# A decoder layer on eight cores: stages around the norms in two column parts, with bf16 weight copies, spread norm steps and independent stores

## The chip, the cores and the metric

The kernel runs one program on all 8 cores of one Trainium2 chip (two dies, cores 0 to 3 and 4 to 7). Each core has 1024 of the 8192 tokens and the whole set of weights. The metric is device time in microseconds (us) of the slowest core, from its first to its last instruction.

The program has a fast and a slow state. In a slow run the cores of one die, sometimes of both, show a lower granted TensorE clock than the others, and the run is up to 20 % longer. A run is called slow when one die is over 1 % longer than the other at a lower clock, or when it is over 1.5 % above the fastest run of the same kernel. Fast runs are compared with fast runs. Where a profile was taken in a slow run, only cores of the die that kept its clock are read, and the text says so.

The engines are TensorE (PE in the profile; PEld is its weight load), VectorE (DVE), ScalarE (ACT), GpSimd (POOL) and SyncE (SP). On the pages a DMA transfer is issued from the queue of an engine, in the kernel before the 688 loads of up weights from GpSimd's (POOLq) and the 32 output stores from SyncE's (SPq).

## The reference, cut to what matters

```python
D_MODEL, SEQ, D_FF, PLE_DIM = 4096, 8192, 11008, 256      # 32 q heads, 4 kv heads of 64, window 128

h = rms_norm(x, norm_mix_pre)
z = h @ w_in                                   # q | k | v | u | g_attn | g_pool
y_attn = sliding_window_attention(q, k, v, sinks) @ w_branch_attn
y_pool = multiscale_pool(u, w_pool, pool_scale) @ w_branch_pool
merged = sigmoid(g_attn) * y_attn + sigmoid(g_pool) * y_pool
x = x + rms_norm(merged @ w_out, norm_mix_post)             # norm after "out"

h = rms_norm(x, norm_ffn_pre)                               # norm before "up"
up = causal_depthwise_conv(h @ w_up, conv_w, conv_b)        # width 3
gate, val = split(up, 2)
x = x + rms_norm((gelu(gate) * val) @ w_down, norm_ffn_post)     # norm after "down"

g = sigmoid(rms_norm(x, norm_ple_gate) @ w_ple_gate)        # norm before "pg"
x = x + rms_norm(g * (p @ w_ple), norm_ple_post)            # last norm: the tail
```

An RMS norm needs the sum of squares over all 4096 channels of a token before any channel can be scaled. On this kernel channels are chunks (32 of 128) and tokens are columns. So between two matmul stages with a norm between them, the last chunk of the first stage has to be done before the first matmul of the second can start, for the same columns.

I use short names for the stages, in order: kv, q (with the attention under it), u (with the pooling), gate (with both branch projections), out, up1, down1, up2, down2, up3, down3 (the MLP in three slices of its 86 chunks), pg (ple gate), tail.

## The kernel before

A small scheduler records every operation with the buffers it reads and writes and turns them into semaphore waits. Each operation waits for the last writer of what it reads, and for the last writer and all readers of what it writes.

```python
def op(self, eng, meth, kw, reads=(), writes=(), dma=None, partial=False):
    deps = {}
    for b in reads:
        ...  # deps of b.w
    for b in writes:
        for d in (b.w, b.r):
            for k, v in d.items():
                if deps.get(k, 0) < v:
                    deps[k] = v          # also where partial=True
    ...
    for b in writes:
        if partial:
            b.w[key] = tid
        else:
            b.w = {key: tid}
            b.r = {}
```

Weights lie in HBM as f32. They are loaded in slabs of 8 x 128 x 128 through a ring of 12 buffers by a DMA from GpSimd's queue that casts to bf16. A job walks over its slabs; for each of the K steps it issues one matmul per column block, here three of 342 columns (1026 in all), with one weight load each.

```python
for kk in range(nk):
    k = k0 + kk
    if job["kpre"] and ci == 0:
        job["kpre"](k)                       # work that has to precede this k step
    ...
    for h, bk in enumerate(ch["banks"]):
        self.O("pe", "matmul", [self.wringB[i]] + rb, [self.psB[bk]], partial=not first,
               out=self.ps[:, bk, 0:ch["n"]], lhsT=self.wring[i][:, kk * 128:(kk + 1) * 128],
               rhs=ch["rhs"](k, h), start=first, stop=last)
    ...
    if job["side"] and cnt // job["side"] > (cnt - 1) // job["side"] and self.side:
        self.side.popleft()()                # side work, here the attention
```

The start, for each of four slabs of 296 columns: all 8 statistics steps (square on ACT, sum by matmul, scaling on DVE), then the K/V matmuls of that slab.

The attention of a chunk of two heads is queued as side work when its q chunk is evicted. Letters are score steps (A, B, one for each head) and value steps (P, Q for this chunk, p, q for the chunk before):

```python
def evac_q(f=f, banks=banks):
    tri_mul(G["q"][f % 3], ...)              # DVE: q rows, 1026 columns
    for c in "A0 p1 B0 A1 q1 B1 A2 p2 B2 q2 A3 B3 P0 A4 B4 Q0".split():
        ...                                  # append the step to B.side
```

The norm between out and up (the one between down and pg is built the same way) is the `kpre` of the first up chunk, over all 1026 columns:

```python
def bar1_k(k):
    ...
    bar1_load()                              # residual rows, 3 buffers in turn
    O("dve", "tensor_tensor", ...)           # m *= rstd
    O("dve", "scalar_tensor_tensor", ...)    # m = m * gain + residual
    O("act", "activation", ..., func=AF.Copy, scale=gains[:, 2, k:k + 1])   # h1[k], bf16
    O("act", "activation", ..., func=AF.Square)
    O("sp", "dma_start", [mB], [x1B[k]], ...)            # store x1
    if n < RESID0:
        O("sp", "dma_start", [msB[n]], [mB], ...)        # fetch a spilled chunk
    tok_ss(...)                              # 9 one-column matmuls: sums of squares per token
```

The tail, after the last matmul, over all 1024 columns and 32 chunks:

```python
outB = Buf("out")
...
for n, f in enumerate(order):
    xload(n + 3)                             # residual x2, 512 KB
    if f < nsp:
        O("sp", "dma_start", [r3B[f]], [rB_], ...)       # spilled result back, 512 KB
    ...
    O("dve", "tensor_tensor", ...)           # r *= rstd
    O("dve", "scalar_tensor_tensor", ...)    # r = r * gain + x2
    O("sp", "dma_start", [rB_], [outB], partial=True, dma="out", out=out_d[f], in_=r)
```

The softmax here doesn't subtract the row's maximum and nothing guards it: scores larger than these inputs give would overflow.

Of the kernel before, what the change touches and what calls it, by code (L numbers as in the profile page):

```python
# [18 lines left out]
H3 = 342  # L19
NK = 1184  # L20
OFF_E = 158
OFF_U = 143
NU = 1041
U3 = 347
NSL = 4
SL = 296
SPLITS = (34, 34, 18)
# [3 lines left out]
RESID0 = 8  # L31
NXS = 3
SCRATCH = 4096

# [119 lines left out]

class Builder:
    def __init__(self):
        nc = self.nc = bass.Bass("TRN2", target_bir_lowering=False, dynamic_dma_scratch_size=SCRATCH)
        self.S = Sched(nc)
        self.live = []
        self.jobs = []  # L160
        self.side = deque()

# [4 lines left out]
    def tile(self, name, off, shape, dt):  # L167
        n = 1
        for s in shape:
            n *= s  # L170
        nb = n * (4 if dt == F32 else 2)
        assert off % 4 == 0 and nb % 4 == 0 and off + nb <= self.arena_bytes, (name, off, nb, self.arena_bytes)
        b = Buf(name)
        b.lo, b.hi = off, off + nb
        keep = []
        for o in self.live:
            if o.lo < b.hi and b.lo < o.hi:
                o.dead = True
                for d in (o.w, o.r):
                    for k, v in d.items():  # L180
                        if b.r.get(k, 0) < v:
                            b.r[k] = v
                if not (b.lo <= o.lo and o.hi <= b.hi):
                    keep.append(o)
            else:
                keep.append(o)
        keep.append(b)
        self.live = keep
        return self.view(off, shape, dt), b


    def tiles(self, name, off, n, shape, dt):
        e = 1
        for s in shape:
            e *= s
        nb = e * (4 if dt == F32 else 2)
        bs = [self.tile(f"{name}_{i}", off + i * nb, shape, dt)[1] for i in range(n)]
        return self.view(off, [n] + list(shape), dt), bs

    def view(self, off, shape, dt):  # L200
        nb = 4 if dt == F32 else 2
        for s in shape:
            nb *= s
        v = self.arena[:, off // 2:(off + nb) // 2]
# [4 lines left out]
        elif len(shape) == 3:  # L209
            v = v.rearrange("p (a b c) -> p a b c", a=shape[0], b=shape[1])  # L210
        return v


    def slabs(self, wname, chunk, sizes, K, base=0):
# [3 lines left out]
        for n in sizes:  # L218
            out.append((wname, off, n, k0))
# [4 lines left out]
    def mm(self, chunks, slabs, side=0, kpre=None, pre=None):  # L224
        self.jobs.append(dict(chunks=chunks, slabs=slabs, side=side, kpre=kpre, pre=pre))
# [4 lines left out]
    def chunk(self, banks, n, K, rhs, rb, evac):  # L230
        return dict(banks=banks, n=n, K=K, rhs=rhs, rb=rb, evac=evac, done=0)

    def load_next(self):
        if self.nload >= len(self.allslabs):
            return
        wname, off, nk, k0 = self.allslabs[self.nload]
        i = self.nload % NS
        self.nload += 1
        src = self.dram[wname][off:off + nk * 16384].rearrange("(p m) -> p m", p=128)
        self.O("pool", "dma_start", [], [self.wringB[i]], dma=f"wr{i}", out=self.wring[i][:, 0:nk * 128], in_=src)  # L240

    def run_jobs(self):
        self.allslabs = [s for j in self.jobs if "slabs" in j for (ci, s) in j["slabs"]]
        self.nload = 0
        self.ncons = 0
        for job in self.jobs:
            if "fn" in job:
# [4 lines left out]
            cnt = 0  # L252
            for ci, (wname, off, nk, k0) in job["slabs"]:
# [5 lines left out]
                for kk in range(nk):  # L259
                    k = k0 + kk  # L260
                    if job["kpre"] and ci == 0:
                        job["kpre"](k)
                    first, last = ch["done"] == 0, ch["done"] == ch["K"] - 1
                    rb = ch["rb"](k)
                    for h, bk in enumerate(ch["banks"]):
                        self.O("pe", "matmul", [self.wringB[i]] + rb, [self.psB[bk]], partial=not first,
                               out=self.ps[:, bk, 0:ch["n"]], lhsT=self.wring[i][:, kk * 128:(kk + 1) * 128],
                               rhs=ch["rhs"](k, h), start=first, stop=last)
                    ch["done"] += 1
                    cnt += 1  # L270
                    if job["side"] and cnt // job["side"] > (cnt - 1) // job["side"] and self.side:
                        self.side.popleft()()
# [9 lines left out]
def build_nc():  # L282
    B = Builder()
    nc, O = B.nc, B.O

# [3 lines left out]
    def dscr(name, shape, dt=F32):  # L289
# [4 lines left out]
    pT_d = din("pT", [128, 2 * T])  # L294
    B.dram = dict(
        w_in=din("w_in", [D * 12800]), w_pool=din("w_pool", [4 * 512 * 512]), w_ba=din("w_ba", [2048 * D]),
        w_bp=din("w_bp", [2048 * D]), w_out=din("w_out", [D * D]), w_up=din("w_up", [D * 2 * DFF]),
        w_down=din("w_down", [DFF * D]), w_pg=din("w_pg", [D * D]), w_ple=din("w_ple", [256 * D]))
    gains_d = din("gains", [128, 6 * NCH])
    conv_d = din("convp", [128, 172 * 4])  # L300
    pscale_d = din("pscale", [128, 16])
    sinks_d = din("sinks", [128, 16])
    corr_d = din("corr", [128, 4 * 18])
    mask_d = din("mask", [128, 512], BF16)
    mask0_d = din("mask0", [128, 132], BF16)
    identb_d = din("identb", [128, 128], BF16)
    out_d = nc.dram_tensor("out", [NCH, 128, T], F32, kind="ExternalOutput").ap()
    mg_d = dscr("mg_s", [30, 128, NE], BF16)
    ms_d = dscr("mix_s", [RESID0, 128, NE])
    x1_d = dscr("x1_s", [NCH, 128, T])  # L310
    yp_d = [dscr(f"yp{i}_s", [NCH, 128, T]) for i in range(2)]
    x2_d = dscr("x2_s", [NCH, 128, T])
    r3_d = dscr("r3_s", [16, 128, T])

    st = ExitStack()
    with st:
        def sb(name, shape, dt):
# [4 lines left out]
        gains = sb("gains", [128, 6, NCH], F32)  # L322
        convp = sb("convp", [128, 172, 4], F32)
        pscale = sb("pscale", [128, 16], F32)
        esink = sb("esink", [128, 16], F32)
        corr = sb("corr", [128, 4, 18], F32)
        maskn = sb("maskn", [128, 512], BF16)
        mask0 = sb("mask0", [128, 132], BF16)
        identb = sb("identb", [128, 128], BF16)
# [3 lines left out]
        sst = sb("sst", [128, 9], F32)  # L333
        rA = sb("rA", [128, NK], F32)
        diag = [sb("diag0", [128, 128], F32)[:], rA[:, 1028:1156]]
        rB = sb("rB", [128, NE], F32)
        constB, sstB, rAB, rBB = Buf("const"), Buf("sst"), Buf("rA"), Buf("rB")
        diagB = [Buf("diag0"), Buf("diag1")]
        B.arena_bytes = ((nc.sbuf_bytes_remaining if not callable(nc.sbuf_bytes_remaining)
                          else nc.sbuf_bytes_remaining()) - 64) // 64 * 64  # L340
        B.arena = sb("arena", [128, B.arena_bytes // 2], BF16)
        ps = B.ps = st.enter_context(nc.psum_tensor("ps", [128, 8, 512], F32))
        psB = B.psB = [Buf(f"ps{i}") for i in range(8)]
        tile = B.tile


        def ld(dst, src):
            O("sp", "dma_start", [], [constB], partial=True, dma="cst", out=dst, in_=src)

        ld(gains[:].rearrange("p a b -> p (a b)"), gains_d)  # L350
        for dst, src in ((pscale[:], pscale_d), (esink[:], sinks_d), (corr[:].rearrange("p a b -> p (a b)"), corr_d),
                         (maskn[:], mask_d), (mask0[:], mask0_d), (identb[:], identb_d),
                         (convp[:].rearrange("p a b -> p (a b)"), conv_d)):
            ld(dst, src)
# [3 lines left out]
        O("dve", "memset", [], [sstB], ap=sst[:], constant=1.0)  # L358

        def tri(b0, n=H3):  # L360
            return ps[:, b0:b0 + 3, 0:n]
# [7 lines left out]
        TRI = ((0, 1, 2), (3, 4, 5))  # L369
        trc = [0]  # L370

        def next_tri():
            trc[0] ^= 1
            return TRI[trc[0]]

        PAIRS = ((0, 1), (2, 3), (4, 5), (6, 7))
        prc = [0]

        def next_pair():
            prc[0] = (prc[0] + 1) % 4  # L380
            return PAIRS[prc[0]]

        def bufs(banks):
            return [psB[b] for b in banks]
# [935 lines left out]
```

## Time and profile before

| | |
|---|---|
| runs of the listing | 7780.94, 8340.58 and 7171.13 us; median 7780.94 |
| profiled run (fast), core by core | 7145 to 7193 us |
| TensorE busy on the slowest core | 6692 of 7193 us |

Two of the three listed runs are slow. The fast time is 7171.

The page of the slowest core (core 1) starts with the busy time of each engine and the span in 40 equal slices. A digit is the busy share of a slice in tenths, PEclk is the granted TensorE clock in tenths.

```profile
...
PE 6692.4 (93%) x41700; PEld 4047.1 (56%) x41700; DVE 1885.3 (26%) x1931; ACT 757.9 (11%) x937; POOL 1035.7 (14%) x1943
...
PE   6889999999999968999999999999999999977980
...
PEclk9999999999999987999999999999999999988995
DMA  6334555555569555444446654444577644677546
...
```

TensorE is above 90 % in most slices. The dents are at the start, at slices 15 and 16, at slice 36, and in the last two. The chain of work that ended last, from the same page, agrees:

```profile
...
PE 91%; DMA 6%; DVE 2%; ACT 1%; issue 1%; SPq 0%; POOL 0%; DVEq 0%; ACTq 0%; POOLq 0%
...
```

For the sizes I cut the span of core 3, which ran undisturbed, at the borders of the stages. The borders come from counting matmuls in program order in the trace. The rows of this table of windows are: start, q, u, gate, out, the 174 us after out, the middle, the 175 us after down3, the rest of pg, tail. Columns: the window, its length, then busy time (and instructions) of PE, PEld, DVE, ACT, POOL, then the clock, the DMA share and GB/s.

```profile
...
0.00:168.30 168.30, 100.23 (x660) 66.23 (x661) 56.14 (x173) 42.77 (x45) 28.02 (x34) 0.93 0.66 164
168.30:526.60 358.30, 318.94 (x2186) 202.52 (x2184) 122.55 (x282) 169.37 (x350) 33.28 (x63) 0.95 0.30 47
526.60:796.60 270.00, 260.62 (x1740) 170.15 (x1739) 95.14 (x105) 30.10 (x46) 40.11 (x76) 0.99 0.44 67
796.60:2157.50 1360.90, 1359.51 (x9266) 901.72 (x9264) 201.46 (x165) 73.27 (x69) 204.81 (x388) 1.00 0.55 86
2157.50:2625.60 468.10, 455.28 (x3090) 301.26 (x3087) 45.61 (x38) 72.32 (x70) 68.09 (x129) 0.99 0.56 90
2625.60:2800.00 174.40, 87.26 (x632) 50.14 (x632) 89.90 (x82) 70.66 (x71) 6.85 (x13) 0.62 0.73 225
2800.00:6384.70 3584.70, 3567.71 (x21697) 2115.62 (x21696) 1004.25 (x860) 160.88 (x153) 573.29 (x1086) 1.00 0.54 94
6384.70:6560.00 175.30, 119.77 (x645) 50.12 (x646) 92.18 (x83) 78.14 (x77) 17.44 (x33) 0.72 0.84 240
6560.00:6957.20 397.20, 391.42 (x1801) 176.71 (x1798) 99.22 (x81) 57.07 (x54) 63.90 (x121) 0.99 0.49 83
6957.20:7154.00 196.80, 0.00 (x0) 0.00 (x0) 78.62 (x64) 3.46 (x3) 0.00 (x0) 0.50 0.59 192
...
```

Length minus PE busy is TensorE's idle time: 68 us in the start, 39 in q, 9 in u, 87 after out, 56 after down3, 197 in the tail, 37 in the rest. Together 493 us of 7154. Where TensorE comes and goes, the mean clock of the window falls too (0.62 and 0.72 in the two norm windows). Part of that fall is the idle time itself, which is recorded at 0.50 (the last row, where TensorE is busy for 0.00 us), so how much the lower clock adds to the cost of the norms was not worked out.

On core 1, the slowest one, 162 us right after the first norm (from 2784.7 us on) ran at a clock of 0.81; core 3 has no such stretch. This makes part of the dent at slice 16 of the page above and of the 39 us by which core 1 is longer.

What a norm waits for is told by the chain of waits of core 1, in order of time (start, duration, what):

```profile
...
2701.76 6.88 DMA sb_arena<-xr
...
2708.73 1.30 DVE sb_arena L138
...
2710.50 7.20 DMA sb_arena<-xr
```

A residual load of 7 us lands, one VectorE operation follows, then the next load is issued and takes 7 us. The loads and the arithmetic take turns. The norm after down3 has the same pattern with loads of 4 to 6 us.

In the attention the hole stands at each q eviction. The timeline of core 1 (start, duration, engine, operation; in brackets the idle time before it and who ended it):

```profile
...
367.33 0.56 DVE L138 TENSOR_TENSOR sb_arena<-ps,sb_arena 64x386 bf16<-64x386 f32 x1 [1.89 <-ACT sb_arena L138]
367.92 1.23 DVE L138 TENSOR_TENSOR sb_arena<-ps,sb_rA 128x1026 bf16<-128x1026 f32 x1
...
369.40 0.32 PE L138 MATMUL ps<-sb_arena 128*128 128x130 bf16 x2 [2.71 <-DVE sb_arena L138]
...
371.42 1.92 PE L138 MATMUL ps<-sb_arena,sb_wr 128*128 128x342 bf16 x6
...
```

The q eviction (1.23 us) waits in VectorE's queue behind a multiply of the step before it, and the first score matmuls wait for it, 2.71 us. Six 342-column matmuls then take 1.92 us, where six such took 1.04 us a little earlier in the same trace. The granted clock is 0.50 for 3.4 us from 370.3 us on, and 1.00 before and after. The array had been idle for 2.71 us before the score matmuls. What sets the moment of the fall is not shown.

In the tail about two thirds of the chain is DMA; VectorE has 18 % of it:

```profile
...
7007.14 3.68 DMA out<-sb_arena
...
7010.89 4.28 DMA out<-sb_arena
...
7095.55 5.38 DMA sb_arena<-r_s
...
```

### The profile page before, as it was taken

Reading aid. Unit: us, or ns where it says so; the run is one execution under the profiler, and the core shown is the slowest. Engines: PE = TensorE matmul, PEld = TensorE weight load, DVE = VectorE, ACT = ScalarE, POOL = GpSimd, SP = SyncE. Lnnn points to the kernel's source line nnn. Section 1 sums busy time; section 2 is a strip of 40 time slices with the busy share of each in tenths; the row PEclk is TensorE's granted clock in tenths of the full one; section 3 lists DMA queues with packets and bytes.
Section 4 is the critical chain, followed back from the end, with each engine's and each line's share of the span. In section 5 each row is a group of like instructions: output and inputs, shape, how many; then the busy total and the mean of one; then the engine's idle time right before and its main releaser. Section 6 shows DMA issues by size and latency. Waiting matters only on the chain.

```text
span 7193.1 us, 100231 instructions; the slowest of 8 cores (7145.0 to 7193.1 us)
## 1 busy us (share of the span) xinstructions
PE 6692.4 (93%) x41700; PEld 4047.1 (56%) x41700; DVE 1885.3 (26%) x1931; ACT 757.9 (11%) x937; POOL 1035.7 (14%) x1943
## 2 busy tenths in 40 slices
PE   6889999999999968999999999999999999977980
PEld 4556666666666644666664456666644566433440
DVE  3333211111110024333330013333300233343223
ACT  2441000000001122000000000000000000122110
POOL 1001111111111100111111111111111111111110
PEclk9999999999999987999999999999999999988995
DMA  6334555555569555444446654444577644677546
GB/s 155 48 45 67 77 81 82 82 82 81 81 113 120 75 127 160 70 75 75 75 78 113 111 96 76 75 75 75 89 148 151 109 75 75 122 183 169 95 68 202
DMA packets 343309, 711.99 MB, mean 99 GB/s; under 512 B 38736, under 2 KB 57424, under 8 KB 340816
## 3 DMA queue, kind: packets, MB, share of 16 engines
q0 software_dynamic: 278928, 480.90, 45.7%
q1 hardware_dynamic: 63936, 224.68, 9.4%
q8 instruction: 338, 5.54, 0.3%
q14 instruction: 107, 0.88, 0.0%
HBM read 1083.94 MB, written 102.26 MB: 165 GB/s over the span
## 4 chain that ended last, share of the span: by engine, by line
PE 91%; DMA 6%; DVE 2%; ACT 1%; issue 1%; SPq 0%; POOL 0%; DVEq 0%; ACTq 0%; POOLq 0%
PE ps L138 91%; DVE sb_arena L138 2%; DMA sb_arena<-x_s 1%; DMA out<-sb_arena 1%; DMA sb_arena<-r_s 1%; DMA sb_arena<-xr 1%; DMA x_s<-sb_arena 1%; DMA sb_arena<-w_in 1%; ACT sb_arena L138 1%; DMA sb_arena<-xs 0%; POOL sb_arena L138 0%; SPq L138 0%; DMA sb_wr<-w_pg 0%; ACT sb_rA L138 0%; ACT L138 0%
## 5 line engine op out<-in xcount | busy, mean ns | idle before, releaser
L138 PE MATMUL ps<-sb_arena,sb_wr 128*128 128x342 bf16 (+2 forms) x39744 | 6504.5, 325 | 28.4 <-ACT sb_arena L138 20.7
L138 PEld LDWEIGHTS ps<-sb_arena,sb_wr 128*128 128x128 bf16 x39744 | 3887.3, 98 | 2533.3 <-issue 44.7
L138 ACT ACTIVATE sb_arena<-sb_arena 128x1024 bf16<-128x1024 f32 (+7 forms) x470 | 443.9, 948 | 4795.6 <-DVE sb_arena L138 4689.9
L138 DVE TENSOR_TENSOR sb_arena<-ps,sb_rB 128x1026 f32<-128x1026 f32 (+1 forms) x204 | 250.2, 1226 | 2201.0 <-PE ps L138 2201.0
L138 POOL DMA_DIRECT2D sb_wr<-w_up x688 | 363.2, 528 | 2213.0 <-PE ps L138 2042.9
L138 DVE TENSOR_TENSOR sb_arena<-ps,sb_arena 128x1024 f32<-128x1024 f32 (+4 forms) x256 | 245.1, 958 | 1121.0 <-PE ps L138 951.5
L138 DVE SCALAR_TENSOR_TENSOR sb_arena<-sb_arena,sb_convp 128x1024 f32<-128x1024 f32 x344 | 442.0, 1285 | 37.7 <-DVE sb_arena L138 2.3
L138 DVE TENSOR_TENSOR sb_arena<-sb_arena 128x1024 bf16<-128x1024 f32 (+6 forms) x251 | 308.4, 1229 | 525.7 <-ACT sb_arena L138 499.9
L138 POOL DMA_DIRECT2D sb_wr<-w_in x384 | 203.0, 535 | 1384.7 <-PE ps L138 1316.7
L138 DVE TENSOR_TENSOR sb_arena<-ps,sb_rA 128x1026 f32<-128x1026 f32 (+4 forms) x136 | 136.6, 1004 | 1008.8 <-PE ps L138 1008.0
L138 POOL DMA_DIRECT2D sb_wr<-w_down x416 | 219.6, 528 | 1001.8 <-PE ps L138 921.7
L138 ACT ACTIVATE sb_arena<-ps 128x512 bf16<-128x512 f32 (+6 forms) x259 | 154.4, 596 | 987.3 <-PE ps L138 980.8
L138 PE MATMUL ps<-sb_arena 128*128 128x296 bf16 (+3 forms) x1216 | 185.9, 275 | 55.3 <-DVE sb_arena L138 45.3
L138 PEld LDWEIGHTS ps<-sb_arena 128*128 128x128 bf16 x1216 | 113.2, 102 | 133.7 <-issue 95.8
L138 DVE SCALAR_TENSOR_TENSOR sb_arena<-sb_arena,sb_gains 128x1024 f32<-128x1024 f32 (+1 forms) x96 | 123.4, 1285 | 132.9 <-DMA sb_arena<-x_s 63.7
L138 PE MATMUL ps<-sb_ones_b,sb_arena 128*128 128x1 bf16 x544 | 25.4, 165 | 142.7 <-ACT sb_arena L138 142.7
L138 DVE TENSOR_SCALAR sb_arena<-sb_arena,sb_convp 128x1024 f32<-128x1024 f32 x172 | 139.9, 814 | 19.6 <-DVE sb_arena L138 1.5
L138 DVE TENSOR_TENSOR sb_arena<-sb_arena,sb_rA 128x1024 f32<-128x1024 f32 (+1 forms) x96 | 117.2, 1220 | 103.9 <-DMA sb_arena<-r_s 81.1
L138 PEld LDWEIGHTS ps<-sb_ones_b,sb_arena 128*128 128x128 bf16 x544 | 21.6, 101 | 183.3 <-issue 181.9
L138 POOL DMA_DIRECT2D sb_wr<-w_out x128 | 67.6, 528 | 383.6 <-PE ps L138 362.6
L138 POOL DMA_DIRECT2D sb_wr<-w_pg x128 | 67.6, 528 | 267.9 <-PE ps L138 245.9
L138 PE MATMUL ps<-sb_arena,sb_ones_b 128*128 128x296 bf16 x128 | 27.0, 355 | 61.5 <-ACT sb_arena L138 33.7
(42 smaller groups left out, 462.9 us busy)
## 6 DMA issues: line engine op xcount, KB each, us to landing
sb_wr<-w_up POOLq DMA_DIRECT2D x688, 256.0 KB, 3.6
sb_wr<-w_in POOLq DMA_DIRECT2D x384, 256.0 KB, 4.3
sb_wr<-w_down POOLq DMA_DIRECT2D x320, 256.0 KB, 4.6
sb_wr<-w_out POOLq DMA_DIRECT2D x128, 256.0 KB, 4.1
x_s<-sb_arena SPq DMA_DIRECT2D x64, 512.0 KB, 5.0
yp_s<-sb_arena SPq DMA_DIRECT2D x64, 512.0 KB, 6.7
sb_arena<-yp_s SPq DMA_DIRECT2D x64, 512.0 KB, 5.5
sb_wr<-w_pg POOLq DMA_DIRECT2D x128, 256.0 KB, 4.4
```

Of the source, the lines that this page charges most:

```text
L138: inst = getattr(engine, fn[0])(**fn[1])
```

## The change

The intent:

1. **Two column parts around a norm.** out, the first 20 up chunks, down3 and pg run once over columns 0 to 511 and then over the rest, so that one part's norm can run under the other part's matmuls. The weights of these stages are therefore read twice.
2. **bf16 copies of those weights.** 116 casting DMAs, spread under the earlier stages, write them to HBM, and the part stages read the copies: half the bytes.
3. **Norm steps spread and pipelined.** A norm is a list of up to 37 small steps, popped one every 14 to 24 k steps. Within a step the multiply, the add, the store and the sum of squares belong to different chunks, and six residual buffers are loaded ahead. Sums of squares become 512-column matmuls.
4. **Statistics of the next K/V slab under the matmuls of the present one**, constants in two loads on another queue.
5. **The attention order**: the first thing after a q eviction is a value step of the chunk before.
6. **Aligned column blocks**: 344, 344, 338 (u: 352, 352, 338; full up: 512, 264, 250) in buffers padded so that every moving operand starts at a multiple of 16 bytes.
7. **The tail** has only the second column part; each output store has an entry of its own, 22 residual chunks are loaded early, nothing is spilled. The MLP is split 29, 29, 28 instead of 34, 34, 18.

```diff
-H3 = 342
+NP = 1032
+H3 = 344
+W3 = (H3, H3, NE - 2 * H3)
-SPLITS = (34, 34, 18)
+SPLITS = (29, 29, 28)
+PARTS = ((0, ((0, 512),)), (504, ((0, 264), (264, 258))))
+RU = 20
...
+    def cast_next(self):
+        dst, do, src, so, n, b = self.casts.popleft()
+        self.O("pool", "dma_start", [], [b], dma=f"cw{self.ncast % 8}", out=self.dram[dst][do:do + n]..., in_=...)
...
+                    if side:
+                        self.due += 1 / side
+                        if self.due >= 1:
+                            self.due -= 1
+                            if self.side:
+                                self.side.popleft()()
...
+        h0 = [alloc(f"h0_{c}", [NK], BF16, shift=4) for c in range(NCH)]
...
+                    if k % 15 == 14 and B.side:              # next slab's statistics
+                        B.side.popleft()()
...
-                for c in "A0 p1 B0 A1 q1 B1 A2 p2 B2 q2 A3 B3 P0 A4 B4 Q0".split():
+                for c in "p1 A0 q1 B0 A1 p2 B1 A2 q2 B2 A3 P0 B3 A4 Q0 B4".split():
...
+        def norm_steps(n, blocks, src, rstd, gp, res, put, gn, hout, rn, xs=None, later=0):
+            ...
+            def step(i):
+                def run():
+                    for lag, fn in ((0, scaled), (1, added), (2, done), (4, ss)):
+                        if 0 <= i - lag < NCH and (hout is not None or fn is not ss):
+                            fn(i - lag)
+                    ...
+            return [start] + [step(i) for i in range(NCH + (4 if hout is not None else 2))]
...
+                    B.side.extend(bar1(hf, G["acc"]))        # after the part's last out chunk
...
-                O("sp", "dma_start", [rB_], [outB], partial=True, dma="out", out=out_d[f], in_=r)
+                b = Buf(f"out{hf}_{k}")
+                outB.append(b)
+                O("sp", "dma_start", [m.b], [b], dma=f"out{k % 8}", out=out_d[k][:, t0:t0 + 512], in_=m.v)
```

(The arena allocator and the renaming of buffers, the larger part of the lines, are cut.)

## The prediction

> All times are for fast runs (before: 7171 us, profiled core 7193); slow runs are not what I predict.
>
> **What bounds it now.** TensorE. The page's busy line gives PE 6692 of 7193 us, the chain of waits is 91% PE. In the table of windows the middle (900 to 2520, 3060 to 6120 us) is dense at clock 1.00. Two things can be won: idle stretches, and ns per matmul.
>
> Idle, from the chain and timeline (core 1):
> - start: the last K/V matmul ends at 166 us for about 80 us of PE work; each 296-column slab's statistics run before its matmuls, not under them.
> - attention under the q projection (186 to 561): 23.5 us per chunk against 17.4 us of PE work. Each chunk has a 5 us hole (363 to 369 us): the q eviction (1.23 us) queues behind the last softmax multiplies, then matmuls run at half clock for about 3 us.
> - out to up norm (2616 to 2775) loses about 145 us; down to gate norm (6402 to 6542) about 115. Each chunk waits for a load, two DVE operations and an ACT square.
> - tail: last matmul 7000, end 7193; 6 us for each of 32 chunks.
>
> Rate: 342-column matmuls start 144 or 148 ns apart in a fixed pattern, 512-column ones 215.8.[...] 347 columns cost about 150.
>
> **What the change does.**
> - Aligns reads: 344+344+338[...] (estimate 144.5 each); u 352+352+338; up 512+264+250 (estimate 436.5 for three, now 440.6). Over 512 q, 512 u, 2048 gate, 1024 branch and 4864 full up k-steps: -48 us, all on the path.
> - Norms in two column parts, steps spread under the other part's matmuls: takes back nearly all of 145+115 us. Adds 28 us of 512-column sums of squares.
> - Part stages need a weight slab every 1.7 us: 152 GB/s, against 75 now. bf16 copies halve the reads; 116 casting copies (2 MB read, 1 MB written each) hide under earlier stages, DMA share there rising from 0.5 to 0.7-0.8.
> - Start: pipelined statistics; DMA (about 34 MB) then binds; q starts near 145, not 170.
> - Attention order: hole per chunk 1-2 us, about -65 us.
> - Tail: half the columns, 22 of 32 residual chunks loaded early: 32 x 1.27 us DVE + 8 us, about 50, not 193: -143 us.
>
> Sum: PE work after, estimate 6490 us at full clock. Plus start idle 65, attention 30, stage boundaries 10, tail 50, part-stage DMA stalls 20, slowest core 15.
>
> **Predicted: 6680 us, range 6600 to 6860. Faster by over 2%: 0.95; within 2%: 0.035; slower: 0.015.**
>
> **Right if** PE is busy about 97%, clock near 1.00 in all slices but the first three; no slice below 9 at the old norm places; last matmul to end about 50 us; 344-column matmuls about 144.5 ns apart.
>
> **Wrong if** part stages are DMA-bound (weights 152 GB/s plus norm loads and stores up to 150 GB/s come near saturation; PE would wait on the weight ring), or casting copies delay weight loads by more than the ring's 12 slabs, or the denser kernel draws a lower clock even in its fast state.

Sum: 6490 + 65 + 30 + 10 + 50 + 20 + 15 = 6680 us. The -48 us of aligned reads, which are within the 6490, rest on my estimates of 144.5 and 436.5 ns alone. The spacings of 144 or 148 and 440.6 ns are measured; that aligned reads would take about the shorter one was not shown at that time. The 17.4 us of TensorE work per chunk are an estimate too; the spacings in the trace of the kernel before (core 3) give about 17.6 (96 x 146.7 + 24 x 109 + 16 x 55 ns). For "near saturation", that trace has 306 GB/s at a DMA share of 0.93 (core 3, 2700 to 2750 us).

## The result, and the profile after

In one session on one chip the changed kernel ran 6697.12, 6669.98, 6669.40 (fast) and 7984.99 us (slow), median 6683.55. The kernel before ran 7171.13 and 7171.16 (fast), 7780.94 and 8340.58 (slow), median 7476.05. Ratios in this document are the mean time of one kernel's fast runs over that of the other's of the same rounds, so not quite the ratio of the medians that are quoted. Here it is 0.931, with a 95 % interval of 0.926 to 0.937: 6.9 % less.

A second series on another occasion gave 6670.78 to 6672.59 us in its four fast runs and a ratio of 0.9295 [0.9275, 0.9314]. Its profile is used for the sizes, since no core was disturbed.

The page of the slowest core of the first series (core 4, 6695.6 us), the same lines as before:

```profile
...
PE 6561.1 (98%) x41283; PEld 4030.5 (60%) x41283; DVE 1975.1 (29%) x2585; ACT 828.2 (12%) x1248; POOL 1352.8 (20%) x2531
...
PE   6999999999999999999999999999999999999996
...
PEclk9998999999999999999999999999999999999998
DMA  7557988899887587688899988556875555589885
...
```

```profile
...
PE 95%; DMA 1%; DVE 1%; ACT 1%; issue 1%; POOL 0%; DVEq 0%; ACTq 0%; SPq 0%; POOLq 0%
...
```

All the dents but the first and the last are gone, and the DMA digits are higher nearly everywhere. The table of windows of the second series, core 7, with these rows: start, q, u, gate, out, all of the MLP, pg, tail.

```profile
...
0.00:145.50 145.50, 95.03 (x655) 65.27 (x656) 57.98 (x181) 43.33 (x45) 29.18 (x42) 0.91 0.82 197
145.50:458.50 313.00, 300.37 (x2188) 195.34 (x2186) 122.87 (x281) 169.04 (x350) 37.45 (x71) 1.00 0.52 81
458.50:722.30 263.80, 256.89 (x1743) 169.29 (x1741) 95.84 (x106) 30.20 (x47) 44.83 (x85) 0.99 0.70 103
722.30:2067.00 1344.70, 1343.25 (x9265) 906.25 (x9263) 202.41 (x165) 73.60 (x69) 230.02 (x436) 1.00 0.77 121
2067.00:2526.00 459.00, 457.31 (x3110) 304.10 (x3109) 85.66 (x128) 122.44 (x197) 137.89 (x257) 1.00 0.66 184
2526.00:6132.00 3606.00, 3600.67 (x22117) 2164.19 (x22116) 1157.28 (x1341) 256.54 (x334) 705.85 (x1331) 1.00 0.70 132
6132.00:6620.70 488.70, 480.59 (x2218) 217.06 (x2215) 212.93 (x319) 132.19 (x206) 166.19 (x310) 1.00 0.77 226
6620.70:6667.20 46.50, 0.09 (x1) 0.00 (x0) 40.56 (x64) 1.32 (x2) 0.00 (x0) 0.51 0.47 181
...
```

TensorE's idle time is now 50 us in the start, 13 in q, 7 in u, 1 in gate, 2 in out, 5 in the MLP, 8 in pg and 46 in the tail: 133 us of 6667, where it was 493 of 7154. Stage by stage, counted from the matmuls in the trace, in us (start and u of the changed kernel are from core 7 of the first series, which ran undisturbed there too; in the second series they are 145.8 and 263.5):

| stage | before, core 3 | after, core 7 | difference |
|---|---|---|---|
| first instruction to first q matmul | 168.3 | 145.5 | -22.8 |
| q with attention | 358.3 | 313.0 | -45.3 |
| u with pooling | 270.0 | 263.7 | -6.3 |
| gate and branches | 1360.9 | 1344.9 | -16.0 |
| out | 468.1 | 458.6 | -9.5 |
| up, three slices | 2555.5 | 2408.9 | -146.6 |
| down, three slices | 1203.5 | 1197.6 | -5.9 |
| pg | 572.5 | 488.5 | -84.0 |
| tail | 196.9 | 46.4 | -150.5 |
| span | 7154.1 | 6667.2 | -486.9 |

In the timeline (core 4 of the first series) the q eviction still takes 1.23 us, but it now lies under other work. Six matmuls of q run while it runs, and the next score matmuls wait 0.39 us:

```profile
...
342.38 1.23 DVE L144 TENSOR_TENSOR sb_arena<-ps,sb_arena 128x1032 bf16<-128x1032 f32 x1
...
342.44 1.03 PE L144 MATMUL ps<-sb_arena,sb_wr 128*128 128x344 bf16 x6
...
343.87 0.32 PE L144 MATMUL ps<-sb_arena 128*128 128x130 bf16 x2 [0.39 <-DVE sb_arena L144]
...
```

And the tail's chain (same core) is VectorE with two operations per chunk, one chunk every 1.26 us:

```profile
...
6650.76 0.75 DVE sb_arena L144 x2
6652.63 0.74 DVE sb_arena L144 x2
...
```

### The profile page after: what moved, and what is told of

Its sections match the earlier page's. It is cut to its first block, busy times and chain, and to the rows that moved or that the text cites. A ratio compares the mean times of both kernels' runs of the same rounds, so it can differ in the third digit from the quotient of the medians.

```text
span 6695.6 us, 104771 instructions; the slowest of 8 cores (6662.8 to 6695.6 us)
## 1 busy us (share of the span) xinstructions
PE 6561.1 (98%) x41283; PEld 4030.5 (60%) x41283; DVE 1975.1 (29%) x2585; ACT 828.2 (12%) x1248; POOL 1352.8 (20%) x2531
## 4 chain that ended last, share of the span: by engine, by line
PE 95%; DMA 1%; DVE 1%; ACT 1%; issue 1%; POOL 0%; DVEq 0%; ACTq 0%; SPq 0%; POOLq 0%
PE ps L144 95%; DVE sb_arena L144 1%; ACT sb_arena L144 1%; DMA sb_arena<-w_in 1%; DMA sb_arena<-xs 1%; POOL sb_arena L144 0%; DVEq L143 0%; ACTq L143 0%; ACT L144 0%; DVEq L132 0%; ACT sb_warm L144 0%; SPq L143 0%; POOLq L169 0%
## 5 line engine op out<-in xcount | busy, mean ns | idle before, releaser
L144 PE MATMUL ps<-sb_arena,sb_wr 128*128 128x512 bf16 (+5 forms) x39744 | 6410.8, 323 | 7.5 <-DVE sb_arena L144 4.4
L144 DVE TENSOR_TENSOR sb_arena<-ps,sb_arena 128x512 f32<-128x512 f32 (+10 forms) x904 | 684.1, 757 | 3995.1 <-PE ps L144 3796.4
L144 ACT ACTIVATE sb_arena<-sb_arena 128x512 f32<-128x512 f32 (+11 forms) x686 | 494.1, 723 | 4627.9 <-DVE sb_arena L144 4511.8
L144 DVE TENSOR_TENSOR sb_arena<-sb_arena 128x512 f32<-128x512 f32 (+8 forms) x545 | 449.6, 837 | 532.6 <-ACT sb_arena L144 503.9
L144 DVE SCALAR_TENSOR_TENSOR sb_arena<-sb_arena,sb_cf 128x1024 f32<-128x1024 f32 (+4 forms) x576 | 593.2, 1031 | 40.8 <-DVE sb_arena L144 0.9
L144 ACT ACTIVATE sb_arena<-ps 128x512 bf16<-128x512 f32 (+7 forms) x291 | 160.2, 550 | 777.4 <-PE ps L144 770.3
L144 PE MATMUL ps<-sb_arena 128*128 128x296 bf16 (+4 forms) x1216 | 182.0, 267 | 30.4 <-DVE sb_arena L144 17.4
L144 DVE TENSOR_SCALAR sb_arena<-sb_arena,sb_cf 128x1024 f32<-128x1024 f32 (+3 forms) x320 | 183.5, 602 | 55.5 <-PE ps L144 20.2
L144 POOL DMA_DIRECT2D sb_wr<-b_down x256 | 137.6, 537 | 283.5 <-PE ps L144 251.2
L144 POOL DMA_DIRECT2D sb_wr<-b_pg x256 | 137.6, 537 | 232.2 <-PE ps L144 215.9
## 6 DMA issues: line engine op xcount, KB each, us to landing
b_out<-w_out POOLq DMA_DIRECT2D x32, 1024.0 KB, 14.1
```

The lines of the kernel that those rows point to most:

```text
L144: inst = getattr(engine, fn[0])(**fn[1])
```

## The experiments

Thirteen more series of runs were made, of ten variants (one of them twice) and twice of the changed kernel itself, all with correct results. Most variants take one part of the change away, do one part alone, or change one number; e8 changes three things at once. The series were run on four occasions and three chips. The kernel before ran beside each of them, and its fast runs were 7167 to 7177 us in most (7180 to 7188 on the chip of e8, e9 and e10; two runs of 7199.52 and 7246.03 also count as fast). The changed kernel itself did not run on the chip of e1, e3, e5 and e7, nor on that of e8, e9 and e10. There a variant is compared with its runs on another chip, where its fast runs alone went from 6670 to 6704 between occasions, so the times of single stages carry these readings better than the totals. "The changed kernel" without a time means the 6670 to 6672 us of its undisturbed series.

### Which part gave the norms: spread steps or column parts (e4)

The column parts and copies stay, but each norm is run as a burst as soon as its part is done.

```diff
                     B.side.extend(bar1(hf, G["acc"]))
+                    B.drain_side()        # the same after bar2 and after the first half of the last norm
```

> The changed kernel with the two column parts kept, but each norm's steps run in one burst between the parts and not spread under the other part's matmuls. My theory (spreading is what hides the norms, parts alone do not): each of the four norms with sums on PE stalls PE for 32 x 1.3 to 1.6 us, 45 to 60 us, and the last one about 25 us through late evictions: whole plus 180 to 260 us. Rival (DVE and ACT catch up while PE works off its queue, half columns alone are enough): whole plus less than 60 us.

Measured: fast runs 6932 to 6940 us, ratio to the kernel before 0.9663, so 265 us more than the changed kernel. On core 7 out takes 580 us instead of 459 (two bursts), down3 503 instead of 396 (two bursts), pg 527 instead of 489; up1 is 6 us shorter, because no steps are left for it. TensorE's longest waits there are for ACT and DVE:

```profile
...
PE ps L144 <- ACT sb_arena L144: 180.1, 159, 8.2
PE ps L144 <- DVE sb_arena L144: 76.1, 49, 38.6
...
```

The same two lines of the changed kernel, same core number:

```profile
...
PE ps L144 <- DVE sb_arena L144: 35.4, 49, 7.5
PE ps L144 <- ACT sb_arena L144: 21.2, 29, 8.3
...
```

So column parts with burst norms gain nothing here: core 7 loses 262 us, and all that the hidden norms bring is some 219 (the sum below). The parts make room, and the spreading uses it. The longest of these waits come at the matmuls that sum the squares, which a burst puts in one place of TensorE's program. The burst norms also have the six residual buffers and the lagged steps, and still cost about 60 us for each part after out. The load chain of the kernel before was thus not the only thing that made its norms dear. (The kernel before with more residual buffers was not run.)

### Whether the copies are needed (e2)

```diff
-  B.slabs("b_out", f, NCH, cast=G["c_out"][f])
+  B.slabs("w_out", f, NCH)
   (the same for b_up, b_down, b_pg; no casting DMAs)
```

> The changed kernel without the bf16 weight copies: the part stages load the float32 weights themselves, with the cast in the load, twice each; the 116 copying DMAs are gone. The prediction's theory (the copies are needed, the part stages would be bound by DMA): float32 reads of 305 GB/s for weights plus up to 150 GB/s of norm traffic[...], so where the norm steps run (out part 1, up part 0, down part 1, gate part 0; about 790 us) the stages grow by a tenth to a third, the whole by 80 to 250 us, PE waiting on DMA of the weight ring. Rival (the ring of 12 slabs and the idle time of the DMA absorb it, the copies only add traffic): whole within 20 us, DMA share lower in the earlier stages.

Measured: fast runs 6935.4, 6937.6 and one of 7016.2, ratio to the kernel before 0.972 [0.9639, 0.9801], so some 265 us more than the changed kernel, a little above the range. Core 7, which is read here, is the least hit (218 us more). On core 7 out takes 486 us, up1 845, down3 464, pg 594, where the changed kernel has 459, 819, 396 and 489. In the stages without casting copies before them the DMA share falls (gate 0.77 to 0.52), and it buys nothing there: gate takes 1345 us in both. Two windows of each, first of e2, then of the changed kernel, both core 7: in out's first part, where no norm runs beside it, and near the start of pg, where the rest of the norm after down3 runs.

```profile
...
2080.00:2300.00 220.00, 219.22 (x1085) 106.03 (x1084) 24.24 (x36) 44.34 (x71) 66.54 (x126) 1.00 0.99 155
6170.00:6300.00 130.00, 110.46 (x484) 45.97 (x484) 45.61 (x70) 36.28 (x58) 36.75 (x71) 0.99 1.06 197
...
```

```profile
...
2080.00:2300.00 220.00, 219.22 (x1058) 103.37 (x1057) 24.68 (x36) 43.08 (x69) 67.99 (x127) 1.00 0.52 151
6140.00:6270.00 130.00, 130.00 (x604) 58.99 (x603) 73.73 (x112) 65.80 (x103) 45.03 (x85) 1.00 0.95 274
...
```

In the first row the f32 weights take the DMA share to 0.99, and TensorE is still full (219.22 of 220 us) with 155 GB/s landed, nearly all of it weights. With a norm beside it the share is 1.06, and TensorE is idle for 15 % of the window. Its waits (us in total, times, longest) say for what:

```profile
...
PE ps L144 <- DMA sb_wr<-w_pg: 66.1, 57, 3.4
PE ps L144 <- DMA sb_wr<-w_down: 48.8, 55, 2.1
...
```

The copies do not pay by making the part stages possible at all, but by leaving room for the norm's own loads and stores. The same bytes landed take twice the DMA share when they come from f32 (0.99 against 0.52 at 155 and 151 GB/s). Whether that is due to the double bytes read or to the cast on the way was not separated.

### The attention order alone (e3)

```diff
-  "p1 A0 q1 B0 A1 p2 B1 A2 q2 B2 A3 P0 B3 A4 Q0 B4"
+  "A0 p1 B0 A1 q1 B1 A2 p2 B2 q2 A3 B3 P0 A4 B4 Q0"
```

> The changed kernel with the old order of the attention steps. In its q stage a chunk takes 20.0 us, in the kernel before 23.5 us. My theory (the order alone closed the hole at each chunk's start): the q stage goes back from 313 us to about 350 to 358 us, the first step of each chunk waits about 2.7 us for the q eviction again, and matmuls run at half clock after it. Rival (the hole shrank through aligned reads, evener counting of the steps or finer softmax tiles): q stage 313 to 325 us. Other stages unchanged within 2 us.

Measured: fast runs 6719.96 and 6719.76 us. q takes 357 us instead of 313, u 267 instead of 264, and the later stages are unchanged. In its trace the first score matmuls again wait 2.73 us for the q eviction. So the order alone closes the hole.

### Statistics before their matmuls again (e7)

```diff
-                    if k % 15 == 14 and B.side:
+                    if False:                        # all steps run at the slab's end
```

> The changed kernel with the input norm's statistics of each slab run after the slab before, not under its matmuls. Prediction's theory (pipelining brings the q stage forward, DMA then binds): q starts at 165 to 170 us instead of 145. Rival (the earlier start came from the shorter constant loads alone, 7 us, and DMA binds in both): q starts at 146 to 152 us. Rest of the stages unchanged.

Measured: fast runs 6692.5 to 6695.2 us, 23 us more. q starts at 164 to 168 us instead of 146, and everything after it is moved by that.

### Alignment of the moving operand (e1)

The h0 buffers are shifted so that their reads start at 0, 4, 8 or 12 bytes past a multiple of 16, in turn with the chunk number. Nothing else is changed.

```diff
-        h0 = [alloc(f"h0_{c}", [NK], BF16, shift=4) for c in range(NCH)]
+        h0 = [alloc(f"h0_{c}", [NK], BF16, shift=4 * ((c + 1) % 4)) for c in range(NCH)]
```

> The changed kernel with one edit: the 32 tiles of the normalised input start at byte offsets 4, 8, 12 and 0 by turns, so the moving reads of the q, u and gate matmuls start at byte 0, 4, 8 or 12[...], by the chunk k. In the changed kernel all start at 0: 344 columns 145.8 ns from start to start, 338 columns 143.3.[...] The gate stage then grows from 1345 us by about 10 us, the whole by about 15 us. Rival A (alignment does nothing, the width alone sets the time): 145.8 and 143.3 at all offsets, gate stage within 2 us. Rival B (any unaligned start costs the same): 338 is slower at 4, 8 and 12 as well.

(The theory was an assumption of mine about what a read costs, which no run shows. By it 344 columns would have taken 145.8 ns at offset 0 and about 149 at 4, 8 and 12, and 338 columns 143 to 144 at every offset. The 10 us for gate and the 15 for the whole come from these numbers.)

Measured: gate 1352 us instead of 1345 on the undisturbed cores, q and u 1 us more each. The one fast run took 6684.63 us, the cores of the undisturbed die in the profile 6674 to 6678. Mean start-to-start times of the gate's three matmuls on core 0, in ns (from each one's start to the next one's):

| read starts at (mod 16) | 344 columns | 344 columns | 338 columns |
|---|---|---|---|
| 0 | 145.05 | 145.06 | 142.64 |
| 4 | 147.5 | 148.3 | 145.9 |
| 8 | 145.0 | 148.3 | 145.85 |
| 12 | 145.0 | 148.7 | 146.0 |

The changed kernel has 145.8, 145.8 and 143.3 in all four cases. A first block may start early after a slow triple and catch up, which was not shown, so sums are safer: the four rows together are 1753.5 ns, 438.4 per triple, against 435.0 in the changed kernel. That is 3.4 ns on average over four rows of which three are unaligned, so about 4.5 ns for an unaligned triple. In the kernel before, where no triple was wholly aligned, it is 440.0, 5 ns more. Times 2048 k steps the 3.4 ns make the 7 us measured.

Alignment is real. But the theory that I had tested is wrong. By it a 338-column read would have taken 143 to 144 ns from each of the four offsets, and yet from 4, 8 and 12 it takes 145.85 to 146.0 ns, 2.5 to 2.7 ns more than the 143.3 ns of the changed kernel. What fits better is a cost for every read that does not start on a multiple of 16 bytes. Why the first block of offsets 8 and 12 shows none of it, catching up or something else, is open.

### The stores of the tail (e5, e6)

e5 gives all output stores of the changed kernel one shared entry again.

```diff
-        outB = []
+        outB = [Buf("out")]
-                O("sp", "dma_start", [m.b], [b], dma=f"out{k % 8}", ...)
+                O("sp", "dma_start", [m.b], outB, partial=True, dma=f"out{k % 8}", ...)
```

> The changed kernel with one shared buffer entry for all output stores, so that each store waits for the landing of the one before, as in the kernel before. My theory now (seen only after the result): in the kernel before, the shared entry chained the stores at about 4.1 us each, and half of the tail's gain comes from the independent stores: the tail goes from 46 us to 100 to 115 us (32 stores of 256 KB, 3 to 3.5 us each). Rival, which is what my prediction said (half the columns and early loads make the tail): tail 46 to 52 us.

Measured: fast runs 6710.0 to 6724.3 us, about 45 more. The tail takes 71 to 77 us instead of 46, pg 495 to 499 instead of 489. VectorE is done at the same time as before, but the stores then land one after the other, every 2.1 to 2.5 us, the last one some 30 us later. The mechanism is the one expected and the size is not. A 256 KB store, alone in flight here, lands in 2.05 to 2.4 us, and I had counted 3 to 3.5 from the 512 KB stores of the kernel before, which take 3.68 to 4.32 us in its tail. How much of the 2.05 to 2.4 us is a fixed cost was not separated here.

e6 does the same the other way round: the kernel before, with independent stores only.

```diff
-        outB = Buf("out")
+        outB = [Buf(f"out{f}") for f in range(NCH)]
-  O("sp", "dma_start", [rB_], [outB], partial=True, dma="out", out=out_d[f], in_=r)
+  O("sp", "dma_start", [rB_], [outB[f]], dma=f"out{n % 8}", out=out_d[f], in_=r)
```

> The kernel before with one part of the change alone: output stores that do not wait for each other. My theory: of the tail's 195 us the first 20 chunks go from 4.1 us to about 3.3 us each (1 MB per chunk in and out by DMA), the last 12, which wait 9 us each for their own spilled tile behind the store in the same queue, stay: tail 170 to 185 us, whole 0.1 to 0.4% faster. Rival (the chain of stores is the tail's limit): tail about 110 to 130 us, whole 1% faster.

Measured: fast runs 7154.3 to 7159.5 us, ratio 0.997 [0.9944, 0.9996]. The tail takes 177 to 181 us (read on the undisturbed die of a slow run) instead of 187 to 200. In the kernel before the stores were only the outermost layer. Under it lie residual loads of about 10 us, loads of spilled results of about 5 us, and twice the arithmetic.

### The early residual loads, and GpSimd in the tail (e9, e10)

e9 loads no residual chunk early (`NKEEP = 22` becomes `NKEEP = 0`).

> The changed kernel with all 32 residual chunks of the last norm loaded when the tail begins, none early. Prediction's theory (early loads are one of the tail's two savings): 8.4 MB more to load beside 8.4 MB of stores, 512 KB per 1.27 us step exceeds the DMA's shown 330 GB/s: tail from 46 to 55 to 65 us. Rival (the loads run ahead of the stores and hide behind the first steps): tail 47 to 51 us.

(The 330 GB/s are what the DMA moves in short windows: 328 in 10 us of the kernel before, core 3 from 2690 us on, and 345 in 10 us of the changed kernel, core 7 of the first series from 2640 us on. Over 50 us both kernels have windows of 306.)

Measured: the tail stays at 46 us on all eight cores, pg takes 494 us instead of 489 on the undisturbed die, spans there 6669 to 6679. No fast run came of it. The early loads gain 5 to 6 us, in pg and not in the tail, so the 55 to 65 us that the prediction's theory expected for the tail were wrong.

e10 (on top of e8, below) gives every third first multiply of the tail to GpSimd.

```diff
-                O("dve", "tensor_tensor", ...)
+                O("pool" if xs is not None and k % 3 == 2 else "dve", "tensor_tensor", ...)
```

> The tuned version, with every third of the tail's first multiplies on GpSimd instead of DVE. If GpSimd runs beside DVE, the tail falls from 46 to about 38 to 41 us (2 x 0.61 + 3 x 0.65 us per three chunks). If the two take turns[...], the tail stays at 45 us or grows.

(Cut are the words that said where the two would take turns, which no run shows.)

Measured: the tail takes 51 us instead of 46. Help from a second engine made it longer. In the trace operations of VectorE that take 0.70 to 0.75 us take 1.75 us while GpSimd works on a multiply of 1.7 us. What makes them longer was not shown.

### A tuned start (e8, e8b)

In the trace of the changed kernel the first weight loads of the ring share the DMA engines with the last x loads (core 7 of the first series: the ring's first loads are issued from 22.7 us on, the last x load at 105.9, and the DMA share is 1.04 from 20 to 100 us). e8 holds the first ring load back until the last x load has landed, sets two constant buffers after the first weight loads, and evicts q in three pieces, so that a score step waits for its piece only.

```diff
+        first = [self.gate] if self.nload == 1 else []
-        self.O("pool", "dma_start", [cast] if cast else [], [self.wringB[i]], ...)
+        self.O("pool", "dma_start", ([cast] if cast else []) + first, [self.wringB[i]], ...)
...
+                for h, (bk, w) in enumerate(banks):
+                    O("dve", "tensor_tensor", [psB[bk], r0.b], [G["qp"][f % 3][h]], ...)     # 344 columns each
```

> A version meant to beat both: the changed kernel, where (1) the first weight slabs of the ring wait until the last input slab has landed, so that 6 MB of weights and one copying DMA no longer compete with the 8 input loads that the start waits for, and the memsets go behind the first loads; (2) the q eviction is three pieces of 344 columns with their own entries, so the first attention step waits for 0.45 us of it and not 1.23 us. Theory from the traces (start is bound by DMA; what is left of the attention hole is the eviction): q starts at 131 to 138 us instead of 146, q stage 298 to 306 us instead of 313, whole 15 to 28 us less than the changed kernel, 6643 to 6655 us. Rival (start bound by statistics on ACT and DVE, hole bound by ACT): less than 6 us.

Measured: q starts at 137 to 139 us (146 before), but takes 310 to 312 us, only 2.5 less. The three pieces were nearly worthless, if the 2.5 us come from them at all. In the trace of the changed kernel the q stage's waits of 150 ns or more sum to only 12 us, so there was little to take. All eight runs had a die at a low clock, three of them both; in the other five the spans on the other die are 6659 to 6665. Nor is it shown that the weight loads delayed the start: e8 also holds back the one copying DMA that was issued among them, and in e2, which has no copying DMAs but the same early weight loads, q starts at 133 to 140 us (mean 137). So the gain at the start may come from that one copy. The two were not separated. e8 was run again beside the changed kernel:

> The tuned start (first gate weight load behind the last x load, constants set after the first weight loads, q rows evicted in three pieces) against the changed kernel on the same chip: from the undisturbed die of the earlier call, the start phase 8 us shorter and the q stage 2.5 us shorter, so 6660 to 6665 us in fast runs where the changed kernel has 6670 to 6672, that is 6 to 10 us less. If the gain is lost to a later wait, the two agree within 3 us.

Measured: fast runs 6690.83, 6687.90 and 6688.40 us, and the changed kernel in the same series 6698.05 to 6703.76. The means differ by 11.5 us, a little more than expected, and both dies show it (die 1 in the profiles: 6656 to 6658 against 6664 to 6668). Three of its six runs are slow, as with the others. It is the fastest version found here.

### Does the dense kernel draw a lower clock? (r0, r1)

> The changed kernel again, as a base for the other runs on this chip and for how often and how much it falls into the slow state: fast runs 6665 to 6700 us, ratio to the fast runs of before 0.930 to 0.934; slow runs, if any, one die at a granted clock near 0.81 and 7950 to 8000 us.

> The changed kernel itself once more, on whatever chip it gets. Theory (the time belongs to the kernel, and the two states to the die's clock): its fast runs are again 6665 to 6690 us and 0.925 to 0.935 of the fast runs of the kernel before, and each run above 6750 us has a die whose mean clock is under 0.99 of the other's; the median of all its runs depends on how many of these there are and is between 6670 and 7600 us. Rival (a denser TensorE load makes the clock fall more often than in the kernel before): at a chip where the kernel before is fast in nearly all of its runs, the changed kernel is not, with a die at a mean clock of 0.97 to 0.98 and times of 6740 to 6830 us, as the three dense variants of the earlier call showed.

Measured for r0: fast runs 6670.78 to 6672.59, three of seven runs slow. Measured for r1, same chip number, later: fast runs 6698.05 to 6703.76, ratio 0.9318 [0.9244, 0.9392], two of six slow. The fast runs of r1 are above the 6665 to 6690 us that were expected, and the slow runs of r0 (7232 to 7554 us) are shorter than the expected 7950 to 8000. The 29 us between the two series are on die 0 only. Its mean clock is 0.989 in r1 and 0.994 in r0; die 1 is the same in both. The loss sits where a norm is hidden: pg takes 513 us instead of 489 on core 0. One window of pg in r1, core 0 (die 0) and then core 5 (die 1), both with TensorE busy throughout:

```profile
...
6120.00:6240.00 120.00, 119.22 (x513) 52.02 (x511) 57.46 (x87) 48.40 (x77) 39.15 (x73) 0.93 0.92 247
...
```

```profile
...
6120.00:6240.00 120.00, 119.22 (x551) 53.81 (x549) 67.73 (x104) 55.22 (x88) 41.28 (x77) 1.00 0.96 267
...
```

The work is the same, the granted clock is 0.93 against 1.00, and 513 matmuls end instead of 551. But 0.93 is a mean. Shorter windows out of this one, with TensorE busy throughout, show core 0 of r1 going back and forth:

```profile
...
6160.00:6168.00 8.00, 8.00 (x32) 3.37 (x31) 5.18 (x8) 4.81 (x8) 2.26 (x5) 0.81 0.78 203
6170.00:6175.00 5.00, 5.00 (x25) 2.27 (x24) 3.85 (x6) 1.94 (x4) 1.07 (x2) 1.00 1.12 285
6177.00:6183.00 6.00, 6.00 (x25) 2.50 (x23) 3.94 (x7) 2.71 (x5) 1.92 (x4) 0.81 1.08 268
...
```

The clock records of all kept traces, on all cores, hold three values and no other: 1.00, 0.81, and 0.50 around idle time. Core 0 of r1 has 28 stretches at 0.81 of 3.7 to 10.8 us each, 191 us in all, every one in a stage with a hidden norm (out, up1, down3, pg). An estimate from this, 191 x (1 - 0.81), is 36 us, and these four stages take 36 us longer there than on core 0 of r0. So the third risk named in the prediction exists at a small size: in r1 die 0 gave less clock where norms were hidden, which cost 0.4 % of the whole time. Why it did so in r1 and not in r0, with the same kernel, is open.

A slow run shows the same 0.81, held longer: on core 4 of the slow run profiled for e1 it is one stretch of 4089 us. Nor does it come only where several engines are dense, or to a whole die. In the first series cores 4 and 5 have one stretch of 161.5 us in u, where no norm runs (u takes 290 and 291 us there instead of 264, hence that run's 6697), and cores 6 and 7 of the same die have none.

In the series of r1 the kernel before has a mean clock of 0.963 on both dies in its fast runs, with one exception of 7246.03 us. On yet another chip, where all eleven runs of the kernel before were fast (7179.7 to 7188.2 us), the dense variants e8, e9 and e10 ran nearly always with die 1 at 0.97 to 0.98 or lower, and had one fast run in 20 (6767.95 us, and that by the rule only, since both dies are at 0.98 in it). This is what the rival in r1's expectation says of a denser kernel. But the changed kernel itself did not run on that chip, so the rival stays open. Apart from that chip, 19 of 33 runs of the kernel before were slow and 6 of 17 of the changed kernel, and I can't tell whether these shares differ.

## Why the prediction was right or wrong

**The number for fast runs was right.** Predicted 6680 for fast runs against 7171, which is 6.85 % less; measured 6669 to 6672 in undisturbed series and 6.9 % less.

**The step that failed is the first sentence: "All times are for fast runs (before: 7171 us, profiled core 7193); slow runs are not what I predict."** The time that was given for the kernel before is the median 7780.94, and that is a slow run, since two of the three runs were slow. Beside this number my 6680 says 14.1 % less, twice what came. I had seen the two states and worked in one of them, but I didn't carry the result to the listed metric, nor say that 610 of the 1100 us between 7781 and 6680 are the state and not the change. What the runs showed in its place: a median of a few runs of this program is decided by how many of them fall into the slow state. The kernel before has listed medians of 7780.94 (3 runs), 7476.05 (4 runs), 7666.01 (7 runs) and 7416 and 7438 (11 runs each), and 7181.8 on the chip where none was slow, all for the same program. The changed kernel falls into that state too (7984.99 us in the first series). The change lowers the time in each state, and does not remove a state. What I should have written is the ratio in the fast state, 0.93, and that the ratio of the listed medians could be anything from 0.80 (6670 to 8340) to 1.11 (7985 to 7171), by chance.

**Part of the closeness is luck.** The prediction summed 6490 us of TensorE work and 190 us for the rest. On core 7 the work is 6534 us (44 more) and the idle time 133 us (57 less, the term for the slowest core included). The two errors nearly cancel.

**The sum, term by term** (us; measured from the stage table and the rates):

| term | predicted | measured | |
|---|---|---|---|
| aligned reads | -48 | about -49 | triples of gate and branches 440.0 to 435.0 ns (3072 k steps), of full up 440.6 to 435.0 (4864), rest from q and u |
| norms hidden (with +28 for the new sums of squares) | -232 | about -219 | up -147 less 27 of alignment, pg -84, out -9, down -6 |
| start | -25 | -23 | e7 alone: +23 |
| attention | -65 | -43 | q -45 less 3 of alignment; e3 alone: q +44 |
| tail | -143 | -150 | e5: +30 in the tail; e6: -15 |
| DMA stalls in part stages | +20 | 0 | part matmuls at 215.8 and 112.5 and 110.0 ns, the 512-column ones as before the change (215.8) |
| slowest core | +15 | +2 to +37 | die clock, above |

- **Aligned reads: right in size, wrong in mechanism.** My theory had a 338-column read cost the same from every offset; e1 shows that it pays as well, 2.5 to 2.7 ns. The size was right because the unaligned times were read from the trace and the aligned ones came out close to my estimates: 145.8 ns for 344 columns (estimate 144.5) and 435.0 for the three of full up (436.5). The other widths keep to one spacing too: 149.2 ns for 352 and 215.8 for 512 columns.
- **Attention: the mechanism was right, the term was mis-sized.** I took 17.4 us of TensorE work per chunk, plus 1 to 2 us of hole. The chunk now takes 20.0 us (q evictions at 302.33, 322.35, 342.38 us) and had 23.7. The waits that are left are almost all under 150 ns: about 0.13 us at each of the side steps, none of which shows in a list of long waits. The estimate of the pure work was too low. e8 shows that a smaller eviction doesn't bring it back.
- **Norms: right**, and e4 and e2 show that both halves of the idea are necessary. Without the spreading the loss is 262 us on core 7, without the copies 218 on core 7 and 265 on the slowest core: as much as the 219 that the norms gained, or more. By this sum half a change here would have been worth nothing.
- **DMA stalls: the risk that I named first didn't come.** The DMA share in the norm stretches is 0.75 to 1.0, and TensorE waits for no weight there. It was a near thing: with f32 weights (e2) the same stretches wait.
- **Tail: right in size, but the cause was only half named.** I credited half the columns and early loads. The early loads are worth nothing in the tail (e9), and the independent stores, which I didn't cost, are worth 30 us of it (e5). The rest is half the arithmetic (32 x 1.26 us) and no spilled results; these two were not separated.
- **The marks that I gave**: PE busy 97 % (98), clock near 1.00 in all slices but the first three (with one slice of 8 at the fourth place in the first series), no slice under 9 at the old norm places, and the tail about 50 us (46) hold. "344-column matmuls about 144.5 ns" was 1 ns too low.

## What to carry to other kernels

When a kernel's time has states, decide first which state the quoted time of the kernel before belongs to, and give the forecast as a ratio within one state; a median of three runs can be a slow run. Here a barrier, the norm, was hidden when three things came together: columns that are independent of it, steps spread over their matmuls, and DMA room for the steps' own traffic. The runs took away the second (e4) and the third (e2); that the first is needed is argued from the structure and was not run. After a change, list the costs that the new structure could pay in (clock, engines that slow each other, DMA share) and look at them where the engines are dense: the longer VectorE operations of e10 (1.75 us instead of 0.70 to 0.75) and most of the lowered clock of r1 (191 us at 0.81 on core 0) showed there, but not the lowered clock of the first series (161.5 us in u). And take a mean clock apart: 0.93 was made of 1.00 and 0.81.
